# Short float32 products among float32r products in a retention and gMLP backbone

## The chip, the cores and the metric

One core of one Trainium2 chip. The metric is the device time of one execution in microseconds, the median over repeated runs. One of the executions is taken apart by the hardware profiler.

## The reference, cut to what matters

Two layers work on 512 latent tokens (x, width 1024) and 256 context tokens (ctx). Layer 0 mixes by bidirectional retention with four heads, layer 1 by a gMLP with spatial gating in chunks of 128 tokens.

```python
hx = rmsnorm(x, norm_g[i]) * (1 + scale_x[:, None]) + shift_x[:, None]
hc = rmsnorm(ctx, norm_g[i]) * (1 + scale_c) + shift_c
# layer 0
qc, kc, vc, zc = retention_project(hc, w_in)
qx, kx, vx, zx = retention_project(hx, w_in)
qx, kx = axial_rope(qx, row, col), axial_rope(kx, row, col)
...
return (o * jax.nn.silu(z)) @ w_out
# layer 1
u = h @ w_in[:, :GM_WIDTH]
v = (h @ w_in[:, GM_WIDTH:2 * GM_WIDTH]).astype(F32)
z = h @ w_in[:, 2 * GM_WIDTH:]
v = v - jnp.mean(v, axis=-1, keepdims=True)
v = v * lax.rsqrt(jnp.mean(v * v, axis=-1, keepdims=True) + NORM_EPS) * vnorm_g.astype(F32)
mixed = jnp.einsum('gij,bnjgc->bnigc', w_s.astype(F32), vg) + b_s.astype(F32).T[:, :, None]
y = u * mixed.reshape(b, l, w).astype(u.dtype)
return (y * jax.nn.silu(z)) @ w_out
```

## The kernel before

All large products run on TensorE in float32r, each as three products of a high and a low part (mm3: low weight by high data, high by low, high by high). split makes the two parts of a tile: ScalarE copies the high part, VectorE subtracts it from the source for the low one. All instructions go through helper objects, so nearly every row of the profile has line 54, and tiles tell them apart.

Large matrix products are taken by quads, two by two blocks of the operands, in the manner of Strassen: seven products of blocks and of sums of blocks in place of eight (names B11, T1, T2, B21, T3, B22, T4), each of 24 float32r products of 128 x 128 weights and 256 columns. A Stream, Q, loads the raw weight tiles (raw) in the order of need and has each split two products ahead into one of four tiles hl. There are two forms. In features, the weights hl stand in the array and the activations (oA, oS, hc, og) move: rows "pst<-oA,hl". In tokens it is the other way round: rows "pst<-hl,oA". (A row names the moving tile first.)

TensorE's instructions run in the order of the text. The stages, with their places in the span:

- Up to about 60 us: norms, the modulation of layer 0 (ada0_mm: cpad columns by ada rows, plain float32, 32 rows wide, four beside each other in the array; ada0_cols: two transposes), and the first quad, written out by hand (plain). The context's products of that quad are six each for a row block k: plain(k, 2); the last three blocks come when kb is 7, then hold("c").
- To about 341 us: the other projections. First a pair of quads in the tokens form, product by product in turn (864 float32r products with the context's beside them), then single quads of the one form or the other. Between them stand pieces of layer 1's modulation: columns multiplies ones by a row block (plain float32, 32 rows wide) and transposes the result.
- To about 545 us: attention for the four heads. Head h has scores (tiles qk), the products with the values (pst<-v,ph and v,pl, 512 columns wide), transposes of the normalised result (gt by ident), and project_out: for each half hf of the tokens and each of eight blocks m, twelve float32r products with og, which VectorE adds to acc. The scores of the next head follow it. Ahead of block m = 4 of the first half (c = 2) stand the transposes of the second half's result (flip), eight on TensorE.
- To about 640 us: the v projection of layer 1 in the tokens form, with its norm's statistics.
- To the end: eight quads for u and z (UZ = 8), in the features form, 168 products each. After product B22 of each, the two spatial products of the quad (s = 0 and 1; four plain float32 products each, wsT by the normalised v, tile vt) go to two PSUM tiles, and gate_f makes from them and from u and z the two high/low tiles for the output projection. After quads 2, 4, 6 and 7 comes out1, with products of 512 columns (rows "pst<-hl,ya", yb, yc).

A plain float32 product (wsT, ones, cpad) runs as two passes, which the trace counts as two matmuls; a transpose is one. PSUM tiles come from two sets: ps, six buffers, and tm, two.

Of the kernel before, what the change touches and what calls it, by code (L numbers as in the profile page):

```python
# [13 lines left out]
P = 128  # L14
# [5 lines left out]
NT = SEQ // P  # L20
# [6 lines left out]
HS = 256  # L27
# [40 lines left out]
def hybrid_kernel(ctx, tc, xT_d, cT_d, cv_d, sv_d, rows_d, ada0_d, adag_d, w_d, rope_d, dec_d, ws_d, id_d, out_d):  # L68
# [13 lines left out]
    def st(shape, tag, dt=F32, bufs=1, name=None):  # L82
        return sb.tile(shape, dt, tag=tag, name=name or tag, bufs=bufs)
# [37 lines left out]
    def pt(shape=(P, 512), tag="ps"):  # L121
        return ps.tile(list(shape), F32, tag=tag, name="pst", bufs=6 if tag == "ps" else 2)

    mm = pe.matmul

    def mm3(out, l, r, first, last):
        (lh, ll), (rh, rl) = l, r
        mm(out, ll, rh, start=first, stop=False, skip_group_check=True)
        mm(out, lh, rl, start=False, stop=False, skip_group_check=True)
        mm(out, lh, rh, start=False, stop=last, skip_group_check=True)  # L130

    def split(hl, src, late=None):
        h, l = hl
        act.copy(h, src)
        low = lambda: dve.tensor_tensor(l, src, f32(h), ALU.subtract)
        if late is None:
            low()
        else:
            late.append(low)
# [185 lines left out]
    def keep(key, src, ks=(0, 4)):  # L325
        k = slice(*ks)
        split((A[key][:, 0, k, :], A[key][:, 1, k, :]), src[:, k, :])

    def features(bank, a, w, fresh, ks=range(4)):

        for kt in ks:
            r = (a[:, 0, kt, :], a[:, 1, kt, :])
            for s in range(2):
                o = s * 512 + kt * P
                mm3(bank[:, s * HS:s * HS + HS], (w[:, 0, o:o + P], w[:, 1, o:o + P]), r, fresh and kt == 0 and s == 0, kt == 3)
# [63 lines left out]
    ones = st([P, P], "ones")  # L399
# [57 lines left out]
    cpad = st([P, KT, 32], "cpad")  # L457
# [56 lines left out]
    def ada0_mm(kb):  # L514
        pa = pt((P, HS), tag="tm")
        rows = ada_w.pop(kb)
        for k in range(KT):
            j = k % 4
            mm(pa[32 * j:32 * j + 32, :], cpad[:, k, :], rows[k // 4][:, j * HS:j * HS + HS], start=(k < 4), stop=(k >= 4))
        e = t2("adae", (P, HS))  # L520
        act.copy(e, pa)
        return e

    def ada0_cols(kb, e):
        pq = pt((P, HS), tag="tm")
        for b in range(2):
            pe.transpose(pq[:, b * P:b * P + P], e[:, b * P:b * P + P], ident)
        s = st([P, 2, 2], "ada_s", bufs=2)
        v = pq.rearrange("p (b g r) -> p b r g", b=2, g=4)
        dve.tensor_reduce(s, v[:, :, 0:2, :], axis=AX.X, op=ALU.add)  # L530
        dve.tensor_tensor(gs0[:, kb, :], s[:, 0, :], adab0[:, 1, kb, :], ALU.add)
        dve.tensor_tensor(sh0[:, kb, :], s[:, 1, :], adab0[:, 0, kb, :], ALU.add)
        dve.scalar_tensor_tensor(gs0[:, kb, :], gs0[:, kb, :], 1.0, g0[:, kb, :], ALU.add, ALU.mult)
# [8 lines left out]
    rope = st([P, 2, SEQ], "rope")  # L542
# [69 lines left out]
    def come(*what, then=None):  # L612


        made = []
        for kb, th in what:
            g, k = divmod(kb, 4)
            r = th // 2
            if r:
                f, h, l = cq[g][:, k, :], hc[:, 0, kb, :], hc[:, 1, kb, :]  # L620
            else:
                name = NAMES[th][g]
                if k == 0:
                    A[name] = st([P, 2, 4, HS], AT_S3.get(name, "o" + name), F32R)
                f, h, l = xq[th, g][:, k, :], A[name][:, 0, k, :], A[name][:, 1, k, :]
            dve.scalar_tensor_tensor(f, f, gs0[:, kb, r:r + 1], rs[th], ALU.mult, ALU.mult)
            made.append((f, sh0[:, kb, r:r + 1], h, l))
        if then:
            then()
        for f, b, h, l in made:  # L630
            act.activation(h, f, AF.Identity, bias=b, scale=1.0)
        for f, b, h, l in made:
            dve.scalar_tensor_tensor(l, f, b, f32(h), ALU.add, ALU.subtract)
# [3 lines left out]
    def plain(kb, th, nhs=range(2)):  # L637

        g = kb // 4
        for nh in nhs:  # L640
            if th == 0 and kb % 4 == 0:
                w0[g, nh] = Q.get(ahead=0)
        if th == 2:
            if kb == 0:
                bank["c"] = pt()
            features(bank["c"], hc[:, :, 4 * g:4 * g + 4, :], w0[g, 0], g == 0, (kb % 4,))
            return
        for nh in nhs:
            if kb == 0:
                bank[th, nh] = pt()  # L650
            features(bank[th, nh], A[NAMES[th][g]], w0[g, nh], g == 0, (kb % 4,))
# [50 lines left out]
    for kb in range(1, 8):  # L702
        if kb == 3:
            Q.upto(4)
        plain(kb, 0)
        if kb + 1 < 8:
            ada0_cols(kb + 1, es)
            come((kb + 1, 0), (kb + 1, 1))
        if kb in (2, 6, 7):
            Q.upto({2: 3, 6: 5, 7: 6}[kb])  # L710
        plain(kb, 1)
        if kb + 2 < 8:
            es = ada0_mm(kb + 2)
        if kb == 2:
            ada0_load(6)
            ada0_load(7)
            Q.cap = None
            Q.pump()
        if kb in (2, 3):
            half_rows(rows_c, kb - 2, sq[2])  # L720
        if kb == 3:
            inverse(sq[2])
        if kb == 4:
            rs[2] = spread(sq[2], "rs2")
        come(*((k, 2) for k in CTX_COME.get(kb, ())))
        if kb == 7:
            hold((0, 0), (0, 1), (1, 0), (1, 1))
            op("S1")
            dve.tensor_tensor(f22, f21, f22, ALU.add)
            dve.tensor_tensor(shb, sh0[:, 0:4, 0], sh0[:, 4:8, 0], ALU.add)  # L730
            for k in range(4):
                shifted(f22[:, k, :], shb[:, k:k + 1], A["S1"][:, 0, k, :], A["S1"][:, 1, k, :])
        for k in CTX_PLAIN.get(kb, ()):
            plain(k, 2)
    hold("c")
    Q.limit = PROJECTED
# [205 lines left out]
    for n, q in enumerate(QUADS[3:]):  # L942
        pr = project(q)
# [123 lines left out]
    def project_out(ws, og, flip, parts, then=None, between=None, prepare=None):  # L1067
        for hf in range(2):
            sl = slice(hf * HS, hf * HS + HS)
            for c in range(4):  # L1070
                w = ws[c]
                if (hf, c) == (0, 2):
                    flip()
                    if prepare:
                        prepare()
                for work in parts:
                    aside(work)
                if then is None and hf == 1 and c < 3:
                    step()
                if between:  # L1080
                    between(hf, c)
                for mi in range(2):
                    m = 2 * c + mi
                    p = pt((P, HS))
                    for kk in range(4):
                        o = kk * 256 + mi * P
                        mm3(p, (w[:, 0, o:o + P], w[:, 1, o:o + P]), (og[hf][:, 0, kk, :], og[hf][:, 1, kk, :]), kk == 0, kk == 3)
                    dve.scalar_tensor_tensor(acc[:, m, sl], p, gate0[:, m:m + 1], acc[:, m, sl], ALU.mult, ALU.add)
                    if then:
                        then(hf, m)  # L1090
# [169 lines left out]
    wsT = st([P, D], "dec", name="wsT")  # L1260
# [94 lines left out]
    vts = {}  # L1355
# [30 lines left out]
    def settle():  # L1386
        while behind:
            behind.pop(0)()

    for i in range(UZ):  # L1390
        got, pms = {}, {}
        prod = Product(features, got.__setitem__)
        for name in SINGLE:
            prod.run(name, Q.get())
            if name == "T2":
                norm_vt(i)
                settle()
            if name == "T2" and i == UZ - 1:
                pair_y = st([P, 2, 2, SEQ], "oA11", F32R, name="yc")
                late_y += [pair_y[:, j] for j in range(2)]  # L1400
            if name == "B22":
                for s in range(2):
                    pm = pms[s] = pt()
                    for n in range(NT):
                        mm(pm[:, n * P:n * P + P], vts[i][:, n, s * P:s * P + P], wsT[:, i * P:i * P + P], start=True, stop=True)
                if i < UZ - 1:
                    load_vt(i + 1)
                gate_f(2 * i + 1, pms[1], {0: got["12"], 1: got["22"]})
        behind.append(lambda i=i, pm=pms[0], mine={0: got["11"], 1: got["21"]}: gate_f(2 * i, pm, mine))
        if i == UZ - 1:  # L1410
            settle()
        if i and i % 2 == 0:
            out1(i // 2 - 1, range(2 if i < UZ - 2 else 1))
# [112 lines left out]
```

## Time and profile before

| | |
|---|---|
| Median of 3 runs | 888.83 us (885.24 to 890.21) |
| The profiled execution | 888.54 us |
| Its span, first to last instruction | 886.8 us |
| TensorE busy | 876.3 us, 6884 matmuls |
| VectorE busy | 712.5 us |
| ScalarE busy | 461.5 us |

A matmul's end is modelled in the trace, and its duration (some 280 ns for 256 columns) is longer than the distance from one start to the next, since matmuls overlap. The rate is read from the starts: the start of a row, less that of an earlier one, over the number of products between them. A row of the timeline gives start, length, engine, line, operation, tiles and count, and in brackets idle time of the engine before it with what ended it. A group row gives count, then busy time in us, mean length in ns, and idle time.

### The profile page before, as it was taken

To read this page: it belongs to the slowest core of one execution; us is meant where nothing else is said; L and a number is where in the kernel's file an instruction comes from. 1 tells how busy PE (TensorE), PEld (TensorE's weight loads), DVE (VectorE), ACT (ScalarE), POOL (GpSimd) and SP (SyncE) were. 2 spreads that over 40 slices of the span, in tenths; PEclk is the share of its full clock that TensorE was granted. 3 is DMA by queue.
4 is the path that set the end of the run, shared out by engine and by line. 5 is a ranking of instruction groups with operands and counts; after the bars stand their busy time and mean duration, and the time that the engine had idled before them with its cause. 6 is when DMAs were issued, how large, how long until landed. Compare 5 with 4: busy or idle time off the path is not lost.

```text
span 886.8 us, 16946 instructions
## 1 busy us (share of the span) xinstructions
PE 876.3 (99%) x6884; PEld 835.0 (94%) x6884; DVE 712.5 (80%) x996; ACT 461.5 (52%) x717; POOL 51.5 (6%) x88
## 2 busy tenths in 40 slices
PE   8999999999999999999999999999999999999997
PEld 7899999999999999998989999999999899899986
DVE  2689967699779877878676689999898488688995
ACT  5464644433554535636265549744666556256434
POOL 0001201002101101000000001011000000000000
PEclk9999999999999999999999999999999999999999
DMA  9943967457577458848345412535445135036212
GB/s 338 403 132 108 291 232 244 161 157 249 188 240 249 137 167 326 289 119 266 136 136 174 156 59 84 197 136 192 134 138 173 42 120 191 24 120 214 60 60 95
DMA packets 75486, 153.81 MB, mean 173 GB/s; under 512 B 7696, under 2 KB 34448, under 8 KB 75408
## 3 DMA queue, kind: packets, MB, share of 16 engines
q1 hardware_dynamic: 68544, 130.69, 45.0%
q0 software_dynamic: 6720, 22.03, 6.5%
q8 instruction: 54, 0.88, 0.4%
q14 instruction: 24, 0.20, 0.1%
q10 hardware_dynamic: 144, 0.01, 0.0%
HBM read 128.58 MB, written 24.12 MB: 172 GB/s over the span
## 4 chain that ended last, share of the span: by engine, by line
PE 91%; DVE 4%; ACT 3%; DMA 1%; issue 1%; SPq 0%; DVEq 0%
PE pst L54 91%; DVE hl L54 1%; DMA xq<-in_xT_dram 1%; ACT f L54 1%; ACT junk L54 1%; DVE raw L54 1%; SPq L54 0%; DVE f L54 0%; ACT hl L54 0%; ACT oA L54 0%; DVE o L54 0%; ACT xs L54 0%; DVE oS L54 0%; DVE xq L54 0%; DVE bns L54 0%
## 5 line engine op out<-in xcount | busy, mean ns | idle before, releaser
L54 DVE TENSOR_TENSOR hl<-raw,hl 128x1024 fp32r<-128x1024 f32 x193 | 234.6, 1220 | 74.8 <-ACT hl L54 74.7
L54 ACT CAST hl<-raw 128x1024 fp32r<-128x1024 f32 x193 | 201.7, 1050 | 141.7 <-PE pst L54 66.3
L54 PE MATMUL pst<-hl,oS 128*128 128x256 f32 x1152 | 135.2, 278 | 0.6 <-DVE snap L54 0.6
L54 PEld LDWEIGHTS pst<-hl,oS 128*128 128x128 f32 x1152 | 133.5, 188 | 1.9 <-ACT snap L54 0.8
L54 PE MATMUL pst<-oS,hl 128*128 128x256 f32 x1104 | 133.6, 280 | 0.7 <-ACT oS L54 0.5
L54 PEld LDWEIGHTS pst<-oS,hl 128*128 128x128 f32 x1104 | 130.2, 189 | 2.3 <-ACT oS L54 1.0
L54 PE MATMUL pst<-oA,hl 128*128 128x256 f32 x936 | 117.4, 281 | 0.2
L54 PEld LDWEIGHTS pst<-oA,hl 128*128 128x128 f32 x936 | 112.0, 189 | 2.6 <-DVE rope_b L54 0.8
L54 DVE TENSOR_TENSOR raw<-raw 128x1024 f32<-128x1024 f32 x92 | 111.7, 1217 | 0.6
L54 ACT COPY snap<-pst 128x512 f32<-128x512 f32 x92 | 53.8, 585 | 97.7 <-PE pst L54 97.3
L54 PE MATMUL pst<-og,hl 128*128 128x256 f32 x768 | 92.4, 281 | 0.0
L54 PE MATMUL pst<-hl,oA 128*128 128x256 f32 x768 | 92.2, 278 | 0.0
L54 PEld LDWEIGHTS pst<-og,hl 128*128 128x128 f32 x768 | 90.5, 189 | 0.8 <-issue 0.2
L54 PEld LDWEIGHTS pst<-hl,oA 128*128 128x128 f32 x768 | 90.0, 188 | 0.2 <-issue 0.2
L54 PE MATMUL pst<-v,ph 128*128 128x512 f32 x192 | 60.1, 394 | 0.0
L54 PE MATMUL pst<-hl,ya 128*128 128x512 f32 (+1 forms) x246 | 59.2, 386 | 0.0
L54 PEld LDWEIGHTS pst<-hl,ya 128*128 128x128 f32 x246 | 45.3, 188 | 9.5
L54 DVE TENSOR_TENSOR snap<-pst,snap 128x512 f32<-128x512 f32 x69 | 47.2, 684 | 4.6 <-PE pst L54 4.4
L54 PE MATMUL pst<-hl,hc 128*128 128x256 f32 x384 | 47.0, 278 | 0.0
L54 PEld LDWEIGHTS pst<-hl,hc 128*128 128x128 f32 x384 | 45.5, 188 | 0.0
L54 ACT CAST ph<-pf 128x512 fp32r<-128x512 f32 x24 | 14.8, 618 | 58.0 <-DVE pf L54 57.6
L54 PEld LDWEIGHTS pst<-v,ph 128*128 128x128 f32 x192 | 36.2, 188 | 7.4
(177 smaller groups left out, 1019.0 us busy)
## 6 DMA issues: line engine op xcount, KB each, us to landing
raw<-in_w_dram SPq DMA_DIRECT2D x224, 256.0 KB, 3.9
bg<-in_adag_dram SPq DMA_DIRECT2D x32, 512.0 KB, 4.2
ada_w<-in_ada_dram SPq DMA_DIRECT2D x16, 512.0 KB, 8.5
raw<-in_w_dram SPq DMA_DIRECT2D x16, 512.0 KB, 4.2
bg<-in_dec_dram SPq DMA_DIRECT2D x12, 512.0 KB, 4.2
v<-snap POOLq DMA_DIRECT2D x16, 256.0 KB, 5.0
z<-snap POOLq DMA_DIRECT2D x16, 256.0 KB, 4.9
v<-v SPq DMA_DIRECT2D x8, 512.0 KB, 4.4
```

Of the source, the lines that this page charges most:

```text
L54: made = op(*args, **kw)
```

## The change

Three edits put plain float32 products at other places on TensorE; no other engine gets or loses an instruction (VectorE, ScalarE and one DMA queue have a few neighbours in another order).

- Ahead of the last ctx row block (k == 7), four products of cpad by the first 256 columns of the rope table, 32 rows wide, go to a PSUM tile that nobody reads.
- In project_out of heads 0 to 2 (the calls without then), in the first half and the fifth block, after the second of its four groups of three, between_modes multiplies ones by ones into a PSUM tile that nobody reads.
- In quads 1 to 7 of u and z the spatial product for s = 0 is issued inside product B22, ahead of its last six float32r products (kt == 3); the one for s = 1 stays behind B22. Quad 0 keeps both behind.

```diff
+    inside = []
+
+    def between_modes():
+
+        pr = pt((P, P))
+        mm(pr, ones, ones, start=True, stop=True)
+
     def features(bank, a, w, fresh, ks=range(4)):
 
         for kt in ks:
+            if kt == 3 and inside:
+                inside.pop(0)()
             r = (a[:, 0, kt, :], a[:, 1, kt, :])
...
         for k in CTX_PLAIN.get(kb, ()):
+            if k == 7:
+                pr = pt((P, HS), tag="tm")
+                for j in range(4):
+                    mm(pr[32 * j:32 * j + 32, :], cpad[:, j, :], rope[:, 0, 0:HS], start=True, stop=True)
             plain(k, 2)
...
                         mm3(p, (w[:, 0, o:o + P], w[:, 1, o:o + P]), (og[hf][:, 0, kk, :], og[hf][:, 1, kk, :]), kk == 0, kk == 3)
+                        if (hf, m, kk) == (0, 4, 1) and then is None:
+                            between_modes()
...
+    def spatial(i, s, pms):
+        pm = pms[s] = pt()
+        for n in range(NT):
+            mm(pm[:, n * P:n * P + P], vts[i][:, n, s * P:s * P + P], wsT[:, i * P:i * P + P], start=True, stop=True)
+
     for i in range(UZ):
         got, pms = {}, {}
         prod = Product(features, got.__setitem__)
         for name in SINGLE:
+            if name == "B22" and i:
+                inside.append(lambda: spatial(i, 0, pms))
             prod.run(name, Q.get())
...
             if name == "B22":
                 for s in range(2):
-                    pm = pms[s] = pt()
-                    for n in range(NT):
-                        mm(pm[:, n * P:n * P + P], vts[i][:, n, s * P:s * P + P], wsT[:, i * P:i * P + P], start=True, stop=True)
+                    if s not in pms:
+                        spatial(i, s, pms)
```

On TensorE at the end of the ctx products (hc is the context's high/low tile, oA_597 and oA_599 are latent tiles, hl the weights):

```order
 L54 MATMUL pst<-oA_597,hl 128x256 x12
 L54 MATMUL pst<-oA_599,hl 128x256 x12
-L54 MATMUL pst<-hc,hl 128x256 x18
+L54 MATMUL pst<-hc,hl 128x256 x12
+L54 MATMUL pst<-rope,cpad 32x256 x4
+L54 MATMUL pst<-hc,hl 128x256 x6
 L54 MATMUL pst<-hl,oA_293 128x256 x24
 L54 MATMUL pst<-hl,hc 128x256 x24
```

The last six of the 18 ctx products now stand behind the new ones, and the pair's products in the tokens form follow them as before.

On TensorE in the second quad of u and z, before:

```order
L54 MATMUL pst<-oA_6392,hl 128x256 x24
L54 MATMUL pst<-oS_6787,hl 128x256 x24
L54 MATMUL pst<-oS_6717,hl 128x256 x24
L54 MATMUL pst<-wsT,vt 128x128 x8
L54 MATMUL pst<-oA_6863,hl 128x256 x24
```

and now:

```order
L54 MATMUL pst<-oA_6403,hl 128x256 x24
L54 MATMUL pst<-oS_6798,hl 128x256 x24
L54 MATMUL pst<-oS_6728,hl 128x256 x18
L54 MATMUL pst<-wsT,vt 128x128 x4
L54 MATMUL pst<-oS_6728,hl 128x256 x6
L54 MATMUL pst<-wsT,vt 128x128 x4
L54 MATMUL pst<-oA_6874,hl 128x256 x24
```

The eight spatial products became two fours with six products of B22 between them.

## The prediction

> **What bounds the kernel now.** I read the page's totals and its chain of waits first.
>
> ```profile
> span 886.8 us, 16946 instructions
> PE 876.3 (99%) x6884; PEld 835.0 (94%) x6884; DVE 712.5 (80%) x996; ACT 461.5 (52%) x717; POOL 51.5 (6%) x88
> PEclk9999999999999999999999999999999999999999
> PE 91%; DVE 4%; ACT 3%; DMA 1%; issue 1%; SPq 0%; DVEq 0%
> ```
>
> TensorE is busy 99% of the span at a full granted clock, and 91% of the chain is its own. No wait can be won. What can still change is how far apart matmuls start. So the next view is the groups of two windows in which TensorE does the same: two neighbouring quads of the gMLP's u/z features, 168 float32r products each, 641.6 to 660.3 us and 662.4 to 681.9 us (busy, mean ns).
>
> ```profile
> L54 PE MATMUL pst<-oS,hl 128*128 128x256 f32 x96 | 11.2, 276 | 0.0
> ...
> L54 PE MATMUL pst<-oS,hl 128*128 128x256 f32 x96 | 11.6, 281 | 0.0
> ```
>
> The same 96 products take 276 ns each in the first quad and 281 ns in the second, with no idle time in either. I call these the short and the long pace. Their start distance comes from rows of the timeline (start, length): short from the tokens products at 199 to 205 us, (204.90-199.46)/48 = 113.3 ns; long from those at 68 to 74 us, (73.81-68.16)/48 = 117.7 ns. The difference, 4.4 ns a product, is the price that all of the gains below use.
>
> ```profile
> 68.16 2.99 PE L54 MATMUL pst<-hl,hc 128*128 128x256 f32 x24
> 73.81 2.99 PE L54 MATMUL pst<-hl,hc 128*128 128x256 f32 x24
> ...
> 199.46 2.88 PE L54 MATMUL pst<-hl,oA 128*128 128x256 f32 x24
> 204.90 1.30 PE L54 MATMUL pst<-hl,oS 128*128 128x256 f32 x10
> ```
>
> What sets the pace? The timeline shows it hold for hundreds of products and turn at places where plain float32 products (wsT, ident, ones, cpad rows) stand between float32r ones.
>
> ```profile
> 639.56 1.95 PE L54 MATMUL pst<-wsT,vt 128*128 128x128 f32 x16
> 641.27 5.70 PE L54 MATMUL pst<-oA,hl 128*128 128x256 f32 x48
> ...
> 660.41 1.95 PE L54 MATMUL pst<-wsT,vt 128*128 128x128 f32 x16
> 662.11 2.13 PE L54 MATMUL pst<-oA,hl 128*128 128x256 f32 x16
> ...
> 681.98 1.95 PE L54 MATMUL pst<-wsT,vt 128*128 128x128 f32 x16
> 683.69 2.98 PE L54 MATMUL pst<-oA,hl 128*128 128x256 f32 x24
> ```
>
> From 641.27 to 660.41 is 19.14 us for 168 products, from 662.11 to 681.98 is 19.87. Every spatial group (8 products, 16 passes in the trace: a float32 product runs as two) turned the pace to the other one. That is what the edit plays on: where such a group stands, and how many there are.
>
> **The change, part by part.** Before, the eight spatial groups turn the pace to short, long, short and so on, and three stretches from one spatial group to the next lie wholly in the long pace (the 19.87 us one, and two like it behind the groups at 724.83 and 789.40), with 24 products more behind the last group.
>
> *The spatial products.* In quads 1 to 7 the 16 passes become 8, six float32r products, 8. If 8 passes turn as 16 do, the first half turns to long, the six run long, the second half turns back, and every quad after quad 0 is short. Gain: 3 x (19.87-19.14) + 24 x 0.0044 = 2.3 us. Cost: the passes are the same, so what is new is one more change of mode in each of seven quads, and six long products (0.03 us). A group takes 1.70 to 1.71 us to the next product; the short quad took 19.14 against 168 x 113.3 = 19.03, so coming out of a group costs up to 0.1. I take 0.05, bounds 0 and 0.1: 7 x (0.05+0.03) = 0.5. Net -1.8. The first half is issued six products (0.7 us) earlier and needs the normalised v, which ACT has finished some 9 us before (ACT's last such instruction for the group at 660.41 began at 648.96), so no wait comes in. That 8 turn like 16 is the assumption; nothing in the trace splits a spatial group, but the lead-in is the same instructions, and the group's own rate is even.
>
> ```profile
> 648.96 0.60 ACT L54 ACTIVATE vt<-vt,nm,rv 128x256 f32<-128x256 f32 x1
> ```
>
> *The ctx products.* Four cpad products (8 passes, 32 columns) now stand ahead of the last six ctx products, in front of the first pair's 864 products in tokens form.
>
> ```profile
> 46.58 1.07 PE L54 MATMUL pst<-ada_w,cpad 128*32 128x256 f32 x16
> 47.58 2.39 PE L54 MATMUL pst<-hc,hl 128*128 128x256 f32 x18
> 49.80 1.58 PE L54 MATMUL pst<-oA,hl 128*128 128x256 f32 x12
> 51.22 0.38 PE L54 MATMUL pst<-ident,adae 128*128 128x128 f32 x2
> 51.36 1.62 PE L54 MATMUL pst<-oA,hl 128*128 128x256 f32 x12
> ...
> 59.68 2.52 PE L54 MATMUL pst<-hl,oA 128*128 128x256 f32 x20
> ...
> L54 PE MATMUL pst<-hl,oS 128*128 128x256 f32 x384 | 46.0, 281 | 0.0
> ```
>
> The cpad group at 46.58 was followed by long features products: 18 starts in 49.80-47.58 = 2.22 us, 123 ns with its lead-in. The two transposes at 51.22 turned to short, and the stretch 51.36 to 59.68 is short. The pair's tokens products from 59.68 on are long: the last row, from 62 to 161 us, has 281 ns. Elsewhere the opposite order holds: long features (180 to 188 us, 281 ns) run straight into short tokens (188.56 on, 276 ns in the window 190 to 229).
>
> ```profile
> L54 PE MATMUL pst<-oS,hl 128*128 128x256 f32 x49 | 6.1, 281 | 0.0
> 188.56 2.90 PE L54 MATMUL pst<-hl,oA 128*128 128x256 f32 x24
> L54 PE MATMUL pst<-hl,oS 128*128 128x256 f32 x144 | 16.8, 276 | 0.0
> ```
>
> So I expect the cpad group to turn the last six features products long, and the 864 behind them to come out short: 864 x 4.4 ns = 3.8 us. Cost: 16 such passes took 47.58-46.58 = 1.00 us, so 8 take 0.5, with 0.2 around them for the change of mode (the 18 long products took 2.22 against 18 x 117.7 = 2.12; the same again at the entrance); 0.5 to 1.2, I take 0.75. Net -3.05. VectorE feeds this stage: busy 88.36 us of 101.7, and the stage becomes 97.9, still 10% slack.
>
> ```profile
> 59.70:161.40 101.70, 101.70 (x866) 101.70 (x865) 88.36 (x108) 54.08 (x73) 15.13 (x23) 1.00 0.61 202
> ```
>
> (Columns: length, then busy time of PE, PEld, DVE, ACT and POOL.) Its new PSUM tile is taken from the two of the tag tm, whose readers are ada0_cols and spread, over by 52 us; rope is loaded in time too.
>
> *The attention's output projections.* In heads 0 to 2 one ones product (two passes) goes in after six products of the fifth output tile.
>
> ```profile
> 372.37 1.03 PE L54 MATMUL pst<-ident,gt 128*128 128x128 f32 x8
> 373.16 17.21 PE L54 MATMUL pst<-og,hl 128*128 128x256 f32 x144
> 390.20 4.41 PE L54 MATMUL pst<-qk 128*128 128x256 f32 x36
> 394.45 0.40 PE L54 MATMUL pst<-v,pl 128*128 128x512 f32 x1
> ...
> 433.98 1.88 PE L54 MATMUL pst<-ada_a,ones 128*128 128x512 f32 x4
> 435.29 6.02 PE L54 MATMUL pst<-og,hl 128*128 128x256 f32 x48
> 441.15 4.24 PE L54 MATMUL pst<-qk 128*128 128x256 f32 x36
> 445.23 0.39 PE L54 MATMUL pst<-v,pl 128*128 128x512 f32 x1
> ...
> L54 PE MATMUL pst<-v,ph 128*128 128x512 f32 x8 | 2.5, 397 | 0.0
> L54 PE MATMUL pst<-v,ph 128*128 128x512 f32 x8 | 2.5, 393 | 0.0
> ```
>
> Behind the transposes at 372.37, og and qk are long: 21.29 us for 180. In head 1 a float32 group at 433.98 makes them short, and short they stay through qk (441.15 to 445.23: 4.08 us for 36, 113 ns) and into that head's value products (393 ns against 397 in the head before). So a turn in head 0 or 2 is worth (174+36) x 4.4 + 60 x 4 ns = 1.15 us, in head 1, whose long part has 90 products left, 0.4: together 2.7. Cost: the two transposes at 51.22 took 0.14 us, and the 12 products behind them (51.36 row and its like) some 0.1 more than their pace; 0.25 each, 0.75 in all; bounds 0.15 and 0.35. In head 1 the group at 433.98 now meets a short pace, and may turn it long: nothing, or 120 x 4.4 + 60 x 4 = -0.8 of the gain; I take half. Net 2.7-0.75-0.4 = -1.55. Two passes turned long to short at 51.22. At 34.83 they did not: the 12 products behind kept the long pace (288 ns, lead-in included). So this part is the least sure.
>
> ```profile
> 34.83 0.38 PE L54 MATMUL pst<-ident,adae 128*128 128x128 f32 x2
> L54 PE MATMUL pst<-oS,hl 128*128 128x256 f32 x12 | 1.7, 288 | 0.0
> ```
>
> *Sum.* 888.54 (this execution's time, 886.8 of span) - 3.05 - 1.8 - 1.55 = 882.1. The execution lies 0.3 us below the median of the three runs shown, 888.83; I leave that out. The VectorE and ScalarE orders differ in a few places in the last stage; neither engine ends a wait of TensorE there, so I cost it at nothing. If that cover went, one split of a weight tile late (1.2 us) would be the size of it.
>
> The Trainium skill speaks against all of this: "TensorE: Matmul & The Clock Gate", section "Step-by-step: what each phase is for", says that TensorE reads weights and moving data through two independent ports, so that loading the next weights takes no bandwidth from the running product. By that rule the place of a float32 product turns nothing and its cost stays, which is the third rival below. The trace disagrees, with 276 against 281 ns for the same 96 products.
>
> **The rivals.** *The ctx group does not turn the tokens products* (the 8 passes leave the features short, as 51.36 to 59.68 were, and the tokens go long again): 882.1+3.8 = 885.9. For it: 8 passes of this form stand nowhere in the trace. Against: the 16 at 46.58 did turn. *The ones products do not turn*: 882.1+1.55+0.75 = 884.4. For it: 34.83. *Nothing depends on place, the products only cost*: 888.54+0.75+0.5+0.75 = 890.5. Against it: three turns in a row at the spatial groups. *Slower: halves of eight always come out long*, as the eight transposes at 372.37 leave the og rows. Then the second half does not turn back, and the 504 features products of 683.69 to 842.91 that are short now go long: 2.2 us; with neither other part working, 890.5+2.2 = 892.7. It decides from the second spatial half of quad 1 on; if the three tokens stages at 188, 265 and 316 us turned as well (792 products, 3.5 us), 896.
>
> **How the numbers follow.** Forecast 0.54; ones fail 0.19; ctx fails 0.14; nothing but cost 0.06; slower 0.07. The range goes down to 879.5: the forecast with the low bounds of the costs (ctx 0.25 less, spatial 0.35, ones 0.3) and nothing given back in head 1 (0.4) is 880.8, and the three runs shown, 885.24 to 890.21, scatter by more than the 1.3 added. It goes up to 887.0, past the ctx rival by 1.1, and leaves the last two cases out. A measurement tells 0.5% from no change, 4.4 us: below 884.4 is faster, up to 893.3 the same. The forecast lies below it nearly always, the ones case half of the time, the ctx case seldom: 0.52+0.1+0.03, 0.65. Slower takes the bad end of the last case and scatter, 0.05; the rest, 0.30, is the same.
>
> **What would show it.** Right: tokens rows from 60 to 161 us at 276 ns; the quads 2 to 7 all near 19.1 us; og rows behind the ones product at 276. Wrong: 281 ns in any of these; or a gap before a pst row that ACT or DVE ends, for which I left no room.

## The result and the profile after

The changed kernel takes 886.99 us (median of 22 runs, 885.73 to 889.21) against 889.0 us of the kernel before (22 runs beside them, 885.24 to 890.55). The ratio is 0.9979, with a 95% interval of 0.997 to 0.9987: a real gain of some 2 us, where 6.4 us were forecast. It lies within the 0.5% that the prediction takes for no change.

The totals and the chain of waits on the page of the changed kernel:

```profile
span 886.5 us, 16978 instructions
PE 873.8 (99%) x6898; PEld 831.7 (94%) x6898; DVE 712.5 (80%) x996; ACT 461.2 (52%) x717; POOL 51.3 (6%) x88
PEclk9999999999999999999999999999999999999999
PE 87%; DVE 5%; DMA 3%; ACT 3%; issue 1%; SPq 0%; DVEq 0%
```

TensorE is still busy 99% of the span at a full clock, and is busy 2.5 us less. The span is only 0.3 us shorter, so waits have come in. This profiled execution took 888.26 us, 1.3 over the median of its kernel; it shows where the parts went, but not their mean.

**The spatial products turned as forecast.** TensorE's timeline in two quads (start, length, tiles, count):

```profile
659.45 1.05 PE L54 MATMUL pst<-wsT,vt 128*128 128x128 f32 x8
660.25 0.95 PE L54 MATMUL pst<-oS,hl 128*128 128x256 f32 x6
661.04 1.06 PE L54 MATMUL pst<-wsT,vt 128*128 128x128 f32 x8
661.86 5.70 PE L54 MATMUL pst<-oA,hl 128*128 128x256 f32 x48
...
680.32 1.05 PE L54 MATMUL pst<-wsT,vt 128*128 128x128 f32 x8
```

From one spatial group to the next are now 680.32-659.45 = 20.87 us. Before, the quad at the long pace had 681.98-660.41 = 21.57, and the short one ahead of it 660.41-639.56 = 20.85. So this quad went to the short pace, and the split costs 0.02 us a quad.

**The ones products turned too.** The same view in the attention's head 0:

```profile
374.49 0.95 PE L54 MATMUL pst<-og,hl 128*128 128x256 f32 x6
375.28 0.38 PE L54 MATMUL pst<-ones 128*128 128x128 f32 x2
375.42 15.90 PE L54 MATMUL pst<-og,hl 128*128 128x256 f32 x138
391.16 4.25 PE L54 MATMUL pst<-qk 128*128 128x256 f32 x36
395.24 0.40 PE L54 MATMUL pst<-v,pl 128*128 128x512 f32 x1
```

Behind the transposes, og and qk take 395.24-374.49 = 20.75 us, ones product included, where they took 21.29.

**The cpad products turned nothing that lasts.** The end of the ctx products, and the group row of the pair's tokens products behind them, in the window 62 to 161 us:

```profile
58.17 1.53 PE L54 MATMUL pst<-hc,hl 128*128 128x256 f32 x11 [0.26 <-DVE hc L54]
59.64 0.64 PE L54 MATMUL pst<-rope,cpad 128*32 128x256 f32 x8
60.21 0.96 PE L54 MATMUL pst<-hc,hl 128*128 128x256 f32 x6
61.01 2.99 PE L54 MATMUL pst<-hl,oA 128*128 128x256 f32 x24
```

```profile
L54 PE MATMUL pst<-hl,oS 128*128 128x256 f32 x384 | 46.0, 281 | 0.0
```

The tokens products have 281 ns, as before. Their 3.8 us did not come. The six ctx products behind the cpad group show where it failed. The last three of them (window 60.85 to 61.0 us) read:

```profile
L54 PE MATMUL pst<-hc,hl 128*128 128x256 f32 x3 | 0.5, 277 | 0.0
```

They had left the short pace for the first products only, and were back in it when the tokens products began.

**The last quad has new waits.** TensorE in the last quad:

```profile
827.00 2.88 PE L54 MATMUL pst<-oS,hl 128*128 128x256 f32 x24
830.36 3.07 PE L54 MATMUL pst<-oS,hl 128*128 128x256 f32 x24 [0.48 <-DVE hl L54]
833.27 2.99 PE L54 MATMUL pst<-oA,hl 128*128 128x256 f32 x24
836.64 5.02 PE L54 MATMUL pst<-oS,hl 128*128 128x256 f32 x42 [0.39 <-DVE hl L54]
...
844.38 3.00 PE L54 MATMUL pst<-oA,hl 128*128 128x256 f32 x24 [0.22 <-DVE snap L54]
```

The waits at 830.36 and 836.64 are for the low half of a weight tile, the third for a result's copy. They are 1.1 us in all, and this quad became 2.0 us longer. About 0.2 us of the rest are the 48 products between the first two waits, which ran at the long pace. The remainder is lost around the waits, which cost more from start to start than the idle time says: the 24 products at 827.00 have 3.36 us to the next row and take 2.72 at the short pace. ScalarE and then VectorE show what was late:

```profile
813.39 0.38 ACT L54 ACTIVATE yz<-pst 128x256 f32<-128x256 f32 x1 [1.92 <-PE pst L54]
816.08 0.60 ACT L54 ACTIVATE vt<-vt,nm,rv 128x256 f32<-128x256 f32 x1 [2.30 <-DMA vt<-vt]
816.59 1.03 ACT L54 CAST hl<-raw 128x1024 fp32r<-128x1024 f32 x1
```

```profile
814.86 0.74 DVE L54 SCALAR_TENSOR_TENSOR ya<-pst,sv,bsb 128x512 f32<-128x512 f32 x1
817.65 1.22 DVE L54 TENSOR_TENSOR hl<-raw,hl 128x1024 fp32r<-128x1024 f32 x1 [2.04 <-ACT hl L54]
```

A normalisation of v waits 2.30 us for its tile's DMA, and the cast of the next weight tile is queued behind it; VectorE, which makes the low half from that cast, stands idle for 2.04 us. Before, ScalarE had the cast first:

```profile
815.74 1.06 ACT L54 CAST hl<-raw 128x1024 fp32r<-128x1024 f32 x1 [2.86 <-PE pst L54]
816.70 0.37 ACT L54 ACTIVATE yz<-pst 128x256 f32<-128x256 f32 x1
817.08 0.60 ACT L54 ACTIVATE vt<-vt,nm,rv 128x256 f32<-128x256 f32 x1
```

VectorE has no room for this: in the 32.02 us of the last quad (815.50 to 847.52 before) it was busy for 31.96.

The table gives each kernel's stages, in us against the profiled execution before. A stage is taken from the start of its first float32r product to that of the next stage's (before: 15.70 and 59.68 for the first two columns, up to 161.44; 340.98, 542.79, 622.61 and 815.50 for the others, up to 847.52). What isn't in it changed by at most 0.09, but for the start of the first stage, which waits for loads and came up to 0.7 later (0.51 in the changed kernel).

| kernel | ratio (95% interval) | to end of ctx | pair's tokens | attention | v stage | seven quads | last quad |
|---|---|---|---|---|---|---|---|
| changed | 0.9979 (0.997-0.9987) | +0.81 | 0 | -1.62 | 0 | -2.02 | +2.00 |
| e1 ctx edit alone | 1.0019 (1.001-1.0029) | +0.79 | 0 | -0.15 | 0 | 0 | 0 |
| e2 attention edit alone | 0.998 (0.9965-0.9994) | +0.11 | -3.50 | -1.61 | +1.49 | 0 | 0 |
| e3 spatial edit alone | 0.9983 (0.997-0.9997) | +0.03 | 0 | -0.15 | 0 | -2.02 | +0.89 |
| e4 2 ones at ctx | 0.9976 (0.9963-0.999) | +0.51 | -3.82 | 0 | 0 | 0 | 0 |
| e5 spatial, v later | 0.9977 (0.9967-0.9988) | +0.06 | -3.51 | 0 | +0.96 | -2.03 | -0.04 |
| e6 spatial, GpSimd | 1.0023 (1.001-1.0037) | +0.09 | -3.51 | -0.16 | 0 | -2.02 | +3.33 |
| e7 1 ones at ctx | 1.0009 (0.9999-1.0019) | +0.29 | 0 | -0.16 | 0 | 0 | 0 |
| e8 8 cpad at ctx | 1.0003 (0.9989-1.0017) | +1.23 | -3.82 | +0.11 | -0.12 | 0 | 0 |
| e9 changed, v later | 0.9982 (0.997-0.9994) | +0.80 | 0 | -1.79 | -0.02 | -2.02 | -0.06 |
| e10 changed, no ctx edit | 0.9971 (0.996-0.9982) | +0.03 | 0 | -1.50 | -0.02 | -2.02 | +0.29 |
| e11 changed, 2 ones at ctx | 0.9948 (0.9928-0.9969) | +0.49 | -3.82 | -1.79 | +0.94 | -2.02 | +1.21 |
| e12 e11, v later | 0.9934 (0.9918-0.995) | +0.47 | -3.82 | -1.89 | +1.49 | -2.03 | -0.06 |
| e13 4 ones at ctx | 0.9964 (0.9952-0.9976) | +0.95 | -3.82 | 0 | 0 | 0 | 0 |
| e14 2 cpad at ctx | 1.001 (1.0001-1.0018) | +0.82 | 0 | 0 | +1.51 | 0 | 0 |
| e15 3 ones at ctx | 1.0008 (0.9999-1.0016) | +0.72 | 0 | 0 | +1.50 | 0 | 0 |

### The profile page after: what moved, and what is told of

It is laid out like the page before. It is cut to its first block, busy times and chain, and to the rows that moved or that the text cites. A ratio compares the mean times of both kernels' runs of the same rounds, so it can differ in the third digit from the quotient of the medians.

```text
span 886.5 us, 16978 instructions
## 1 busy us (share of the span) xinstructions
PE 873.8 (99%) x6898; PEld 831.7 (94%) x6898; DVE 712.5 (80%) x996; ACT 461.2 (52%) x717; POOL 51.3 (6%) x88
## 4 chain that ended last, share of the span: by engine, by line
PE 87%; DVE 5%; DMA 3%; ACT 3%; issue 1%; SPq 0%; DVEq 0%
PE pst L54 87%; DMA xq<-in_xT_dram 2%; DVE hl L54 1%; DVE o L54 1%; ACT f L54 1%; DMA raw<-in_w_dram 1%; DMA vt<-vt 1%; ACT junk L54 1%; ACT hl L54 1%; DVE raw L54 1%; DVE f L54 0%; ACT oA L54 0%; DMA qk<-q 0%; DVE ya L54 0%; ACT xs L54 0%
```

## The experiments

### Each edit alone

**e1_ctx_only**: of the change, only the cpad products ahead of the last six ctx products.

> The kernel before with the ctx edit alone. Theory A (the eight cpad passes leave the last six ctx products in the short pace, and short features run into long tokens products, as in the one execution profiled): the pair's tokens products stay at 281 ns, and only the group's cost is left, about 0.8 us: 889.8 against 889.0. Theory B (in most executions the group does turn the tokens products short, and the profiled one is an exception): a gain of up to 3 us, 886 to 888.

890.43 us (888.85 to 891.1, 12 runs) against 888.73. The 864 products stay at 281 ns, and the edit costs its 0.8 us. The medians are 1.7 apart; of the rest the profile shows 0.68 as a later start of the first stage.

**e2_attn_only**: only between_modes in project_out.

> The kernel before with the ones products in heads 0 to 2 alone. Theory A (the pace of og, qk and the value products turns short behind each ones product and nothing takes it back): 1.6 to 2.0 us less, 887.0 to 887.4. Theory B (later waits take it back): within 0.5 us of before.

887.55 us (883.39 to 888.71, 12 runs). The attention's stages are 1.6 us shorter. In the profiled execution (885.2 us) the pair's tokens products, which this edit doesn't touch, are short as well; what follows from that stands below. The sum of the attention is known to some 0.2 us only: e1, e3, e6 and e7 have -0.15 or -0.16 there without an edit in it.

**e3_spatial_only**: only the split of the spatial products.

> The kernel before with the spatial products of quads 1 to 7 split, nothing else. Theory A (all quads run short and TensorE is 2 us ahead when the last quad begins, where VectorE is behind with its weight splits and takes about all of it back): 0 to 0.7 us less, 888.3 to 889.0, with idle rows ended by DVE hl between 826 and 846 us. Theory B (the waits of the last quad belong to the one execution profiled): 1.8 to 2.0 us less, 887.0.

887.06 us (883.31 to 890.28, 12 runs). The quads give the same 2.02 us, and the last quad takes 0.89 back, with the same order on ScalarE:

```profile
815.93 0.60 ACT L54 ACTIVATE vt<-vt,nm,rv 128x256 f32<-128x256 f32 x1 [1.67 <-DMA vt<-vt]
816.43 1.04 ACT L54 CAST hl<-raw 128x1024 fp32r<-128x1024 f32 x1
```

So the give-back belongs to the spatial edit.

### Which products turn the pace at the ctx place

These kernels are the kernel before with one insertion at the place of the ctx edit. e4 has:

```diff
         for k in CTX_PLAIN.get(kb, ()):
+            if k == 7:
+                pr = pt((P, HS), tag="tm")
+                for j in range(2):
+                    mm(pr[:, j * P:j * P + P], ones, ones, start=True, stop=True)
             plain(k, 2)
```

e7 has range(1), e15 range(3) and e13 range(4) (the latter two with j % 2 for the columns of pr). e8 and e14 have the change's cpad products, in range(8) (with j % 4 for the rows of pr) and range(2).

> The kernel before with two products of ones by ones (four passes, 128 columns, all 128 rows) at the place of the ctx edit's cpad products. Theory A (the kind and number of passes decide; four or a multiple of it of full-width passes turn short features long, as the halves of the spatial groups did): the last six ctx products long, the pair's 864 tokens products short (276 ns), 864 x 4.4 ns less 0.45 us: 3.4 us less, 885.6. Theory B (the tokens products are long at this place whatever stands ahead): 281 ns, 0.45 us more, 889.4.

> The kernel before with one product of ones by ones (two passes) at the place of the ctx edit. Theory A (the number of passes decides: four turned, and two are half of a turn): the last six ctx products stay short and the pair's tokens products long (281 ns), 0.25 us more than before, 889.0. Theory B (any full-width float32 product turns): 276 ns, 3.6 us less, 885.1.

> The kernel before with eight cpad products (16 passes) at the place of the edit's four. Theory A (number of passes): as at 46.58 us of the kernel before, where 16 such passes were followed by the long pace, the six ctx products go long and the tokens products short: 3.8 less 1.2 us, 886.1. Theory B (products of 32 columns never turn at this place): 281 ns and 1.2 us more, 890.

> The kernel before, with four products ones by ones (eight passes of 128 columns) ahead of the last six ctx products. Theory A (the number of passes decides: eight at this place leave the tokens products long, as the eight cpad passes did): 276 is not reached, the 864 products stay at 281 ns, and the time is 0.5 to 1.2 us over before. Theory B (the width of the passes decides: 128 columns turn, 32 do not): 276 ns, the pair's tokens products 3.8 us shorter, front +0.9, 885.8 to 886.5.

> The kernel before, with two cpad products (four passes of 32 columns) ahead of the last six ctx products. Theory A (the number of passes decides: four turn): 276 ns in the pair's tokens products, 3.8 us shorter, front +0.5, 885.3 to 886. Theory B (the width decides: 32 columns do not turn): 281 ns, 889.0 to 889.5.

> The kernel before, with three products ones by ones (six passes) ahead of the last six ctx products. Theory A (an odd number of such products leaves the tokens products long, an even number turns them short, as one and two did): 281 ns, 889.2 to 890. Theory B (any number from two up turns them): 276 ns, 885.5 to 886.3.

The tokens group of e13, and then that of e15, from 62 to 157 us; some products of e15 already lie behind the window's end:

```profile
L54 PE MATMUL pst<-hl,oS 128*128 128x256 f32 x384 | 44.3, 276 | 0.0
```

```profile
L54 PE MATMUL pst<-hl,oS 128*128 128x256 f32 x364 | 43.7, 281 | 0.0
```

| inserted | passes | weight x moving columns | tokens products | median, before beside it |
|---|---|---|---|---|
| 1 ones (e7) | 2 | 128 x 128 | 281 ns | 889.22, 888.65 |
| 2 ones (e4) | 4 | 128 x 128 | 276 ns | 885.56, 888.73 |
| 3 ones (e15) | 6 | 128 x 128 | 281 ns | 890.85, 890.21 |
| 4 ones (e13) | 8 | 128 x 128 | 276 ns | 886.65, 890.21 |
| 2 cpad (e14) | 4 | 32 x 256 | 281 ns | 891.04, 890.21 |
| 4 cpad (e1) | 8 | 32 x 256 | 281 ns | 890.43, 888.73 |
| 8 cpad (e8) | 16 | 32 x 256 | 276 ns | 888.9, 888.65 |

The kernel before stood at 890.21 beside e13 to e15, 1.2 to 1.6 over the other comparisons, so those medians are held against it and not against the expectations' times. The profiles of e14 and e15 have the v stage 1.5 us longer, which would explain such a shift; of the kernel before no profile was taken then.

The number of passes alone doesn't decide (e13 against e1, both eight), nor is more always enough (e15 against e4). Of ones products, two and four turn the tokens products short, one and three don't: the alternation that e15 was to tell. Two and four cpad products don't turn them. Of e8's ten runs five lie between 886.10 and 887.90 and five between 889.90 and 891.01: its profiled execution, 886.33 us, is one of the lower five, so 276 ns seems to be one of two outcomes there; the other was not profiled. e4 has two of its twelve runs at 889.21 and 889.63, the others up to 886.55.

**One count fits all seven kernels.** In the trace four cpad products start 6 to 7 ns apart, and then their second passes in the same way: they run beside each other. Two of them take as long as four: 0.55 us from their start to the next ctx product in e14, 0.57 in e1. Counted as passes one after another, the ones products make 2, 4, 6 and 8 and the cpad products 2 (e14), 2 (e1) and 4 (e8): four and eight turn (e8's four not in every run), two and six don't. This count was made after the runs, and none of them tests it; by it, twelve cpad products, six passes in turn, should leave the pace alone. It is also no rule for other places: in head 0 one ones product, two passes, turned the long pace short.

**What is turned are the six ctx products.** The last three of them in e4 (window 60.12 to 60.27 us):

```profile
L54 PE MATMUL pst<-hc,hl 128*128 128x256 f32 x3 | 0.5, 281 | 0.0
```

The tokens products then have the other pace, and so it is in all 17 profiles: where the last ctx products have 276 to 278 ns the tokens products have 281, and where those have 281 or 282 these have 276.

### The last quad

**e5_spatial_held**: e3, and in the last quad ScalarE's normalisations of v are ordered behind a later cast of a weight tile.

```diff
         h, l = hl
         act.copy(h, src)
+        casts.append(act.recent)
...
             if name == "T2":
+                order, act.last = act.last, casts[-2] if i == UZ - 1 else act.last
                 norm_vt(i)
+                act.last = order
                 settle()
```

> The split of the spatial products alone, with ScalarE's normalisation of v for the last quad ordered behind the weight copies of the last quad's products up to B21. Theory A (what gives the gain back is the order on ScalarE: the normalisation waits for its load at the head of ScalarE's queue, with a weight copy and VectorE's half of it behind): no idle row of TensorE between 820 and 846 us ended by DVE, all of the 2.0 us kept, 886.7 against 888.7. Theory B (VectorE is full in that stretch, 27.94 of 28 us in the kernel before, and no order helps): 0.9 us or more still given back, 887.6 to 888.

886.66 us (884.37 to 889.37, 12 runs) against 888.65. The last quad gives nothing back (-0.04), and TensorE waits for no hl tile in it. In its ratio it can't be told from e3.

**e6_spatial_pool**: e3, with two elementwise passes of out1's third output group (its function drain) on GpSimd to give VectorE room.

```diff
-            dve.tensor_tensor(s, s, Q.gate[:, h], ALU.mult)
-            dve.tensor_tensor(s, s, xs, ALU.add)
+            nc.gpsimd.tensor_tensor(s, s, Q.gate[:, h], ALU.mult)
+            nc.gpsimd.tensor_tensor(s, s, xs, ALU.add)
```

> The split of the spatial products alone, with the two elementwise passes of the third output group (times the gate, plus the residual) on GpSimd in place of VectorE: 16 passes of 0.68 us off VectorE, half of them in the stretch before the last quad. Theory A (order on ScalarE): VectorE still idles for 1.4 us behind the weight copy, but catches up with the time that it won: some 0.5 to 0.9 us better than with the split alone. Theory B (VectorE is full): the same, and no idle row at all, 886.7. Both fall if GpSimd is slower than what waits for it: then later than the split alone.

891.1 us (886.9 to 893.62, 12 runs): slower. TensorE now waits longer in the last quad, both for a weight tile and for a result to be read out:

```profile
833.65 5.18 PE L54 MATMUL pst<-oS,hl 128*128 128x256 f32 x42 [0.81 <-DVE hl L54]
...
842.95 3.02 PE L54 MATMUL pst<-oA,hl 128*128 128x256 f32 x24 [1.64 <-DVE snap L54]
```

The late cast is still there (VectorE waits 0.69 us for it), and VectorE got slower. Rows of GpSimd, and then of VectorE:

```profile
825.68 2.27 POOL L1320 TENSOR_TENSOR o<-o,gateb 128x512 f32<-128x512 f32 x1
...
832.50 2.15 POOL L1321 TENSOR_TENSOR o<-o,xs 128x512 f32<-128x512 f32 x1
```

```profile
813.54 1.23 DVE L54 TENSOR_TENSOR hl<-raw,hl 128x1024 fp32r<-128x1024 f32 x1 [0.69 <-ACT hl L54]
...
824.48 0.68 DVE L54 TENSOR_TENSOR o<-pst,o 128x512 f32<-128x512 f32 x1
825.08 3.95 DVE L54 TENSOR_TENSOR hl<-raw,hl 128x1024 fp32r<-128x1024 f32 x2
831.18 4.55 DVE L54 TENSOR_TENSOR hl<-raw,hl 128x1024 fp32r<-128x1024 f32 x2
```

While GpSimd works, from 817.86 to 834.65 us, the low half of a weight tile takes VectorE 1.6 to 2.3 us in place of 1.22, and so do its other passes with both inputs in SBUF; passes with an input in PSUM (o<-pst,o) stay at 0.68. TensorE's waits are for VectorE's passes, none for GpSimd's. Of the expectation, theories A and B missed; that it falls if GpSimd is too slow was said, but not that VectorE itself slows down.

**e9_after_held**: the whole change with e5's edit.

> All three edits as in the change, with one thing more: in the last quad ScalarE's four normalisations of v stand behind the casts of the weight tiles again. Theory A (what the change gives back in the last quad, +2.0 us in its profile, is ScalarE's order alone): the last quad from its spatial group on takes 32.0 us as before, TensorE shows no waits ended by DVE hl there, and the median is 0.7 to 2.0 us under the change's 887.0, that is 885.0 to 886.3. Theory B (the last quad is longer because VectorE has too little slack once the quads run at the short pace): the segment stays 1 us or more over 32.0, the median 886.5 to 887.3.

886.68 us (885.62 to 888.17, 12 runs). The cast is first again on ScalarE, 1.03 us behind the first row, and VectorE follows it without a wait:

```profile
812.81 0.38 ACT L54 ACTIVATE yz<-pst 128x256 f32<-128x256 f32 x1 [1.92 <-PE pst L54]
813.84 1.05 ACT L54 CAST hl<-raw 128x1024 fp32r<-128x1024 f32 x1 [0.65 <-DVE raw L54]
```

```profile
814.93 1.22 DVE L54 TENSOR_TENSOR hl<-raw,hl 128x1024 fp32r<-128x1024 f32 x1
```

The last quad takes 31.97 us, as theory A said, so ScalarE's order is the cause. The pairs that differ in this edit alone agree: +0.89 and -0.04 in e3 and e5, +1.21 and -0.06 in e11 and e12. The median is not where A had it (885.0 to 886.3) but 0.4 above, and its ratio can't be told from the change's. Without the order edit the profiles of e3, e10, e11 and the change give back 0.89, 0.29, 1.21 and 2.00 us: the change's profile shows a large case. What the order costs on average isn't resolved: each pair's ratios lie within one another's intervals.

### The parts together

**e10_no_ctx**: the change without its ctx edit. **e11_ones2_all**: the change with e4's two ones products in place of the four cpad products. **e12_ones2_held**: e11 with e5's order.

> The change without its edit in the last ctx products; the other two edits and the give-back in the last quad stay. Theory A (the ctx edit only costs its 0.8 us, and takes away the occasional executions in which the pair's tokens products come out short): the median is 0.8 us under the change's, 885.7 to 886.4, with single runs as low as 883. Theory B (the ctx edit is worth something together with the others): 887 or more.

> The change with its four cpad products ahead of the last six ctx products replaced by two products ones by ones (four passes). Theory A (the edits are independent, so their terms add): ctx +0.5, the pair's tokens products -3.8 (276 ns a product in place of 281), attention -1.6, quads -2.0, last quad +0.9 to +2.0: 882.6 to 884.2. Theory B (a turn early on shifts all that follows: a later stage that was short, as the v stage at 542 to 622 us, comes out long and gives 1 to 1.5 us or more back): 884.5 to 886.5, with that stage longer in the profile.

> The change with two products ones by ones in place of the four cpad products, and with ScalarE's normalisations of v in the last quad behind the casts of the weight tiles. Theory A (the terms add): 0.7 to 2.0 us under the kernel without the second edit, 881.0 to 882.8, the fastest of all. Theory B (a turn early on is given back by a later stage): 883.5 or more.

e10: 886.11 us (884.81 to 888.12, 12 runs), as theory A had it, though no run came as low as 883. e11: 883.52 us (882.02 to 887.64, 6 runs), also A's, though its v stage did come out 0.94 longer, as B said. e12: 883.0 us (881.33 to 883.72, 6 runs) against 888.86, a ratio of 0.9934 (0.9918 to 0.995). That is 0.2 over A's bound, and in the profiled execution the v stage is 1.49 longer, as B said. It is the fastest kernel of the study, and the only one at which the forecast gain is nearly all there (5.9 of 6.4 us):

```profile
span 881.4 us, 16969 instructions
PE 870.3 (99%) x6894; PEld 829.5 (94%) x6894; DVE 711.6 (81%) x996; ACT 460.7 (52%) x717; POOL 51.4 (6%) x88
```

## Why the prediction was wrong

**What bounds the kernel, and the two paces: right.** All that was won was won in start distances, and a turned stretch gave what 4.4 ns a product says: 3.82 us for the 864 tokens products in e4, against 3.8 forecast.

**The spatial products: right, with a cost set too high.** -2.02 against -1.8. Every half of eight turned the pace; the cost was 0.02 us a quad for which 0.08 were taken. The rival in which halves always come out long fell.

**The attention: right in the sum.** -1.62 against -1.55, of other parts. Heads 0 and 2 gave 0.92 and 0.94 (0.53 each up to the end of qk's first 36, the rest in what follows), their ones products counted in. In head 1 the group at 433.98 (now 434.63) did not turn the pace back, so the 0.4 set aside weren't taken by it; but that head lost 0.40 elsewhere, at a weight load that waits for VectorE:

```profile
417.15 5.41 PEld L54 LDWEIGHTS pst<-og,hl 128*128 128x128 f32 x47 [0.45 <-DVE og L54]
```

TensorE's og products start at 416.75 against 416.35 before, VectorE's og pass at 416.42 against 415.56: TensorE had gained 0.5 us on VectorE, and waits for it. That is the "gap" for which the prediction left no room. In e9's profile the wait is absent, and this head loses 0.25.

**The step that failed**: "I expect the cpad group to turn the last six features products long, and the 864 behind them to come out short". The cost was right (0.75 forecast, 0.81 measured; e1 alone is slower by its interval), the gain of 3.8 was nil. The step has two halves. The second held in every profile: behind long ctx products the tokens products are short. The first failed: the six ctx products behind the cpad group came out short (277 ns), so the 864 came out long (281 ns). The step took the group of 16 passes at 46.58 as proof for one of eight. The runs showed that at this place it depends on what is inserted: two or four ones products turn the pace; one or three ones products, and two or four cpad products, do not; eight cpad products do in about half of the runs, going by their times. Why such a group turns the pace stays open. The rival for this case, 885.9 us, is the one that came; the median lies 1.1 above it. That the median, 886.99, is still inside the range that ends at 887.0 is luck: by the terms the range was reached with the largest of the three gains missing.

**The second step that failed**: "neither engine ends a wait of TensorE there, so I cost it at nothing". ScalarE's new order in the last quad delayed a weight tile, by up to 2.0 us (1.2 was the size given for it). It had been read that nobody waited there before; not weighed was that VectorE was busy for 31.96 of 32.02 us in that stage, so that a pause of 2 us on it can't be made up.

By terms the profile gives 0.81 - 1.62 - 2.02 = -2.8 us, and the last quad takes 0.3 to 2.0 of it back: -2.5 to -0.8, around the measured -2.0.

The Trainium skill, "TensorE: Matmul & The Clock Gate", section "Step-by-step: what each phase is for", says that loading the next weights takes no SBUF read bandwidth from the running product. The prediction drew from it a rival in which place turns nothing. e13 against e15 speaks against that rival: the same 864 products are 3.82 us apart, behind four ones products and behind three. Whether the read ports have a part in it no run shows.

## What to carry to other kernels

Where a stream of equal matmuls runs at two start distances in one trace, the difference can be won by a few plain products between, but whether a certain group turns the pace must be measured for its kind, its number and its place; one like it elsewhere in the trace proves nothing. Take the cheapest group that turns in nearly all runs, and look at single runs, not the median alone. And where an edit reorders an engine off the critical path, read the slack of that engine and of the one that it feeds in that very stage before it is costed at nothing: here 0.06 us in 32. Moving passes to GpSimd need not relieve VectorE: in e6 those that stayed got up to 1.1 us longer each.

## What the runs showed that was not expected

**A stretch can come out either way without an edit near it.** e2, e5 and e6 touch nothing ahead of 341 us, yet the tokens group of e5, in an execution of 884.37 us, reads:

```profile
L54 PE MATMUL pst<-hl,oS 128*128 128x256 f32 x384 | 44.3, 276 | 0.0
```

That is worth 3.5 us. In these three profiles the last ctx products are long already, behind the wait at 58 us. It fits the spread of the kernel before: 20 of its 22 runs beside the change lie from 888.70 to 890.55 us, two at 885.24 and 885.42; beside e1 to e8, 14 of 70 lie from 885.08 to 887.74, some of them between the two groups, so this stretch isn't the only one that varies. e1, with the cpad products, had no run under 888.85.

**The v stage does the same, behind a wait.** The first 192 products after the 0.3 us wait for VectorE, in the kernel before (the window 542 to 592 us), and then in e12 (537.5 to 588 us):

```profile
L54 PE MATMUL pst<-hl,oS 128*128 128x256 f32 x192 | 22.0, 277 | 0.3 <-DVE snap L54 0.3
```

```profile
L54 PE MATMUL pst<-hl,oS 128*128 128x256 f32 x192 | 22.9, 282 | 0.3 <-DVE snap L54 0.3
```

The long pace there and behind makes the stage 1.49 us longer. At the ctx place, too, a wait of 0.26 us ends just ahead (the row at 58.17). That the pace depends on the moment at which such a wait ends would explain the two outcomes; it is argued, no run sets that moment.

**Weight loads differ by a nanosecond.** The loads of the tokens group have a mean of 188 ns at the short pace (e13) and 189 ns at the long one (e15). That doesn't show whether the loads set the pace or follow it; the mechanism stays open.
